# Two trunk layers on one core: the low part of the feed-forward weights made by an accumulating DMA instead of VectorE

## The chip, the cores and the metric

One core of a Trainium2 chip runs the whole program. The metric is the device time of one execution in microseconds; before the change it is 2593.01 us, the median of 2 runs (2591.31 to 2594.72).

## The reference

Two layers work on 640 tokens of 1024 channels (128 context tokens, 512 latent tokens). Each layer is

```
h += 1/2 * g1 * swiglu(adaLN1(h), ffn1)       # first feed-forward part
h += g2 * (heads(adaLN2(h)) @ w_out)          # mixer: state space, two attentions, Fourier
h += 1/2 * g3 * swiglu(adaLN3(h), ffn2)       # second feed-forward part

def swiglu(x, wg, wu, wd):
    return (jax.nn.silu(x @ wg) * (x @ wu)) @ wd
```

with wg and wu of 1024 x 2816 and wd of 2816 x 1024. The shift, scale and gate of each adaLN come from `silu(cond) @ w_mod + b_mod`, where w_mod is 1024 x 9216 per layer. Everything is float32.

## The kernel before, in words

**Products in three passes.** Each float32 operand is split into two parts of type float32r, a high part (the value rounded) and a low part (the value minus the high part). A product is three matmuls into the same PSUM tile: high x high, high x low, low x high (`mm3`, lines 257 to 265, and the same written out at lines 666 to 668 of `ffn`). The activations x and the hidden values (hh, hl) are split too. The tokens are worked in two halves of 256 and 384.

**The weight stream.** All weights of the feed-forward parts, of the input projection and of the output projection come as one stream of slabs, up to 1 MB each, loaded by SP into three `raw` buffers (`load_upto`). A slab of the gate and up weights holds 8 x 256 columns per partition, one of the down weights 4, 6 or 8 x 256. A slab gives two pieces, each a half of its columns, so a piece reads runs of 128 values (512 bytes) of the slab. `prep_to` (line 193) makes a piece: ScalarE writes the high part `whi` (line 209), VectorE the low part `wlo` (line 210), each contiguous per partition. The pieces lie in a ring of six slots. There are 344 pieces: per feed-forward part 44 of gate and up, and 32 (layer 0's first and second part) or 24 of down; 12 of the projection and 16 of the output per layer. A `raw` buffer is free for the next load when the low part of its second piece is made.

**Order of the work.** `ffn` goes through its chunks: for each of the 128 hidden channels of a chunk (a block: one gate and one up piece, 96 matmuls) both halves, then silu on ScalarE and the product and split on VectorE and ScalarE (lines 677 to 681), then the down product with `res_phase` (line 1551), which adds to the residual hT (line 595). Its last five blocks of channels are done half by half, so that the norm of the first half (`finish_half`, `rstd_from`, `x_prep`) can be made beside the second. `x_prep` (line 535) uses VectorE, ScalarE, and for some blocks POOL (line 561). Python code asks for the pieces ahead of their use (`w`, line 218, with `ahead` = 2); the order on each engine is then set by a scheduler with a timeline of its own, so instructions stand earlier or later than the code writes them.

**The modulation.** Beside the feed-forward parts VectorE multiplies slabs of w_mod (512 KB, tile `wm`) into `mvec` (lines 387 and 389). POOL issues their loads (line 353) into two buffers, so an issue waits until VectorE is done with the slab two before. They run in the first three of the four feed-forward parts; the last has none.

**The tables.** Beside the first chunks of two of the parts, tables of the state-space heads are made and written to DRAM by POOL's queue (tiles est, ft, zs).

Of the kernel before, what the change touches and what calls it, by code (L numbers as in the profile page):

```python
# [10 lines left out]
F32 = mybir.dt.float32  # L11
# [98 lines left out]
class Net:  # L110
    def __init__(self, tc, a, depth=DEPTH, dump=None):
        self.tc = tc
        self.nc = tc.nc
        self.a = a
        self.depth = depth
        self.dump = dump or {}
        self.es = ExitStack()
        self.n_act = 0
        self.wq = []
        self.raw = {}  # L120
        self.ready = {}
        self.i_use = 0
        self.i_prep = 0
        self.slabs = []
        self.i_load = 0
        self.slab_left = {}
        self.side = []
        self.job = None
        self.job_ns = 0
        self.chunks = CHUNKS  # L130
        self.limit = 0
        self.load_limit = 0
        self.seg = []
        self.mseq = [(l, gi, k) for l in range(depth) for gi in range(9) for k in range(DB)]
        self.m_load = 0
        self.m_use = 0
        self.mslab = {}
        self.mod_bufs = 4
        self.m_limit = 16
        self.m_pace = None  # L140
        self.m_ns = 0
        self.mod_then = None
        self.ahead = 2
        self.fine = False
        self.marks = ()
        self.x = [None, None]

    def pool(self, name, bufs=1, **kw):
# [17 lines left out]

# [1 line left out]
    def add_slab(self, src, pieces):  # L168
# [24 lines left out]
    def prep_to(self, n):  # L193
        while self.i_prep < min(n, len(self.wq), self.limit):
# [11 lines left out]
            with ExitStack() as es:  # L206
                for i in self.marks:
                    es.enter_context(self.tc.issue_after(i.ins))
                self.nc.scalar.activation(hv, v, AF.Copy)  # L209
                self.nc.vector.tensor_tensor(lv, v, hv, op=OP.subtract)  # L210
            self.ready[self.i_prep] = (hv, lv)
# [6 lines left out]
    def w(self, ahead=2):  # L218
        """Next operand of the stream; keeps `ahead` more in preparation."""
        i = self.i_use  # L220
# [3 lines left out]

# [1 line left out]
    def later(self, ns, f):  # L226
# [29 lines left out]

# [1 line left out]
    def mm3(self, out, pairs):  # L258
# [7 lines left out]

# [1 line left out]
    def setup(self):  # L268
# [36 lines left out]
    def setup_vectors(self):  # L305
        """small vectors: rows of 128, transposed to columns."""
        nc, a = self.nc, self.a
# [33 lines left out]

# [1 line left out]
    def mod_load(self, n):  # L343
# [14 lines left out]
    def mod_step(self):  # L358
        """One slab of w_mod: [128 rows, one of the nine vectors] on the tensor engine while it has nothing else,
        later [256 rows, half of one of the nine vectors] on the vector engine, the sum over partitions at the end."""  # L360
        nc = self.nc
# [66 lines left out]
    def mod_to(self, n, ns=None):  # L428
        """slabs up to n: spread over the coming ns, or what is left of them now."""
        self.m_limit = n  # L430
# [43 lines left out]

# [1 line left out]
    def load_x(self):  # L476
# [26 lines left out]
    def rstd_from(self, ss, c0, n):  # L503
        """ss [P, n] sums of squares per token -> rs_tok columns."""
        nc = self.nc
# [3 lines left out]

# [1 line left out]
    def norm_bc(self, half):  # L511
        """broadcast of rstd over the partitions, in PSUM [P, width]."""
        nc = self.nc
# [17 lines left out]
    def x_norm(self, half, rb, k, x):  # L531
        """h * rstd of one block."""
        self.nc.vector.tensor_tensor(x, self.hT[half][:, k, :], rb[:, 0:HALVES[half][1]], op=OP.mult)

    def x_prep(self, half, l, j, rb=None, xn=None):
        """x = h rstd A + B as two parts; xn: h rstd, where it is there already."""
        nc = self.nc
# [59 lines left out]
    def finish_half(self, half, l, j):  # L597
        """norm of a finished half of the residual, spread over the coming matmuls."""
        self.later(T_SUM, lambda: self.sq_sum(half))
# [8 lines left out]

# [1 line left out]
    def ffn_specs(self, l, nm, chunks):  # L610
# [21 lines left out]
    def ffn(self, l, j, nxt, chunks, e_pro=None):  # L632
        """j: 0 or 2; nxt: (layer, norm) the next phase reads, or None.
        e_pro: the pool of the tables that are made beside the first N_TAB chunks."""
        nc = self.nc
        hps, hp = self.open_pool("hp")
        nf = max(n for _, n in chunks[:N_TAB if e_pro else None])
        for ci, (c0, n) in enumerate(chunks):
# [58 lines left out]
            self.res_phase(n, [(hh[i], hl[i]) for i in range(2)], [(f, f) for f in range(n)], (l, j), nxt if last else None)  # L697
        hps.close()

# [1 line left out]
    def open_pool(self, name, **kw):  # L701
# [18 lines left out]

# [1 line left out]
    def ssm_tables(self, pro, l):  # L722
        """Generator: tables of layer l (E, intra-chunk Toeplitz blocks, F) to DRAM."""
        nc, a = self.nc, self.a
# [75 lines left out]
        def exp_fix(o, x):  # L800
            """e^x from the power of the rounded e and the rest of e."""
            stt(o, x, E_DELTA, zp, OP.mult, OP.mult)
            return tt(o, o, zp, OP.add)
# [57 lines left out]
        for n in (1, 2, 4):  # L861
# [9 lines left out]
            tt(yi, yi, tw[:, 0:n], OP.add)  # L871
        # (a - 1) / lambda
        nr = ts(T(), ap[:, 0, 1], -1.0, None, OP.add)
# [115 lines left out]

# [1 line left out]
    def proj_specs(self, l):  # L991
# [28 lines left out]
    def proj_u(self, l):  # L1020
        """u of the SSM, channels on the partitions, and u of the Fourier group, tokens on the partitions."""
        nc = self.nc
# [33 lines left out]

# [1 line left out]
    def ssm_init(self, l):  # L1058
# [18 lines left out]
    def ssm_te_load(self, l):  # L1077
        """most of E where the third part of the projection will be."""
        te = self.pp.tile([P, 10, 256], F32, name="te5", tag="P2")
# [49 lines left out]
    def ssm_y(self, l, mx):  # L1129
        """Generator over the steps after the scan."""  # L1130
        nc, a = self.nc, self.a
# [88 lines left out]

# [1 line left out]
    def merged_tiles(self):  # L1222
        self.mg = [self.x_tiles(h) for h in range(2)]

    def split(self, src, blk, c0, w, bias=None):
        """hi and lo parts of 128 channels of the merged heads, tokens c0..c0+w."""
        nc = self.nc
# [13 lines left out]

# [1 line left out]
    def fnet_load(self, l):  # L1243
# [53 lines left out]

# [1 line left out]
    def rope_tile(self, X, qr, ti):  # L1299
        """roped queries to qr, roped keys in place."""  # L1300
        nc = self.nc
# [60 lines left out]
    def qk_T(self, X, qr, ck, qt):  # L1362
        """Generator: transposes of queries and keys, four blocks of 128 columns per group.
        qt: roped q of the two query slots, roped k, plain q of the two slots, (ctx q, q, k, cached k)."""
        nc = self.nc
# [3 lines left out]
        def put(i, srcs, nq=4):  # L1369
            """the first nq blocks are queries: scaled by 1/8."""  # L1370
            pt = self.b([P, 4, P], name="qkT")
# [61 lines left out]
    def att(self, X, qt, blk0, mx, cv, PT, exs, sink=None, band=False):  # L1433
        """Latent queries; generator, yields where other work may go.
        PT: the two transposed tiles of a group; exs: function giving a tile for the exponentials."""
        nc = self.nc
# [80 lines left out]

# [1 line left out]
    def out_specs(self, l):  # L1519
# [18 lines left out]
    def out1(self, l):  # L1538
        """Generator: the part of the output projection whose heads are ready."""
        for db in range(DB):  # L1540
# [10 lines left out]
    def res_phase(self, n, xs, order, G, nxt, lead=1):  # L1551
        """y = W^T x, added to the residual, the last four blocks half by half."""
        def one(db, half, wd):
# [33 lines left out]

# [1 line left out]
    def sinks(self, l):  # L1589
# [8 lines left out]
    def mixer(self, l):  # L1598
# [35 lines left out]
        self.limit, self.load_limit = self.seg[l + 1]  # L1634
        # Fourier mixing while the scan runs
        rw = self.rawp.tile([P, RAW], F32, tag="raw", name="qs0")
# [4 lines left out]
        self.weave([self.fnet(l, mx), self.ax_norm(l), gq])  # L1641
        # both attention groups, the end of the state space heads, the first half of the output projection
        rw = self.rawp.tile([P, RAW], F32, tag="raw", name="qa0")
# [40 lines left out]
    def weave_main(self, main, others):  # L1684
        """others: (generator, one step every so many of main, offset)."""
        step = 0
# [15 lines left out]

# [1 line left out]
    def output(self, half):  # L1704
# [120 lines left out]
```

## Time and profile before

| | |
|---|---|
| median of 2 runs | 2593.01 us |
| the profiled execution's span | 2589.3 us |
| PE busy (matmul) | 2517.7 us (97%) |
| VectorE (DVE) busy | 1507.6 us (58%) |
| ScalarE (ACT) busy | 823.6 us (32%) |
| GpSimd (POOL) busy | 387.2 us (15%) |
| DMA queue q1 (issued by SP) | 193.30 MB, 23.7% of 16 engines' span |
| DMA queue q0 (issued by POOL) | 78.00 MB, 10.2% |
| granted TensorE clock, mean | 0.985 |

The profiled execution's own time is 2589.3 us from its first to its last instruction, 3.7 us below the median of the runs. Busy time of PE is modelled, since its matmuls overlap; DMA issues stand under the engine that issues them, and their transfers under the queue. "Idle before" in a group is the time that its engine stood still just ahead of it, with the engine, tile and line that ended it.

### The profile page before, as it was taken

The numbers are of one execution on the slowest core, as the hardware profiler recorded it, in microseconds if no ns is written. First come the engines' busy times: TensorE is split into PE (matmuls) and PEld (weight loads), VectorE is DVE, ScalarE is ACT, GpSimd is POOL, SyncE is SP. The second block draws the span as 40 slices with busy tenths as digits, with TensorE's granted clock in tenths as the row PEclk, the third lists the DMA queues.
The fourth block names the chain that finished last, engine by engine and source line by source line (L and its number), as shares of the span: only waits on it lengthen the run. The fifth ranks groups of instructions, "written<-read, shape, count | busy, mean of one in ns | idle before, by whom it ended". The sixth has DMA issues, their size and how long they took to land.

```text
span 2589.3 us, 41527 instructions
## 1 busy us (share of the span) xinstructions
PE 2517.7 (97%) x17054; PEld 2366.8 (91%) x17054; DVE 1507.6 (58%) x3012; ACT 823.6 (32%) x1547; POOL 387.2 (15%) x782
## 2 busy tenths in 40 slices
PE   5999999999899999999999999999999999999998
PEld 3899999998669899999999999999976799999998
DVE  6888677363667876454456666644546773333333
ACT  3332222242443532222233222223425553222222
POOL 2321111014801211000011001000183010000000
PEclk7999999999999999999999999999999999999999
DMA  7565444231114254333314445432401133222311
GB/s 254 158 182 183 145 147 147 90 101 55 34 35 147 58 168 126 119 111 114 114 50 143 137 125 151 139 106 66 126 18 54 34 98 98 69 82 62 98 49 41
DMA packets 199092, 273.93 MB, mean 106 GB/s; under 512 B 17208, under 2 KB 168472, under 8 KB 198392
## 3 DMA queue, kind: packets, MB, share of 16 engines
q1 hardware_dynamic: 176888, 193.30, 23.7%
q0 software_dynamic: 22016, 78.00, 10.2%
q8 instruction: 134, 2.20, 0.4%
q14 instruction: 54, 0.44, 0.1%
HBM read 256.29 MB, written 14.97 MB: 105 GB/s over the span
## 4 chain that ended last, share of the span: by engine, by line
PE 77%; issue 9%; POOL 7%; DVE 5%; DMA 2%; ACT 1%; SPq 0%; DVEq 0%; POOLq 0%; ACTq 0%
PE gu L261 14%; PE gu L263 14%; PE gu L262 14%; PE y L261 8%; PE y L262 8%; PE y L263 8%; POOL sc L1124 2%; POOL ee L1127 2%; POOL ee L1126 1%; DMA wm<-in_w_mod_dram 1%; POOL sc L1125 1%; DVE wlo L210 1%; DVE xt L551 1%; PE gu L668 1%; PE gu L666 1%
## 5 line engine op out<-in xcount | busy, mean ns | idle before, releaser
L261 PE MATMUL gu<-xh,whi 128*128 128x256 f32 (+1 forms) x2560 | 794.2, 310 | 0.9 <-DVE hx L679 0.9
L263 PE MATMUL gu<-xh,wlo 128*128 128x384 f32 (+1 forms) x2560 | 789.4, 309 | 0.6 <-DVE wlo L210 0.6
L262 PE MATMUL gu<-xl,whi 128*128 128x384 f32 (+1 forms) x2560 | 788.7, 308 | 0.0
L209 ACT ACTIVATE whi<-raw 128x1024 fp32r<-128x1024 f32 (+2 forms) x344 | 328.5, 960 | 875.4 <-PE gu L262 424.8
L210 DVE TENSOR_TENSOR wlo<-raw,whi 128x1024 fp32r<-128x1024 f32 (+2 forms) x344 | 380.2, 1107 | 343.3 <-ACT whi L209 342.9
L261 PEld LDWEIGHTS gu<-xh,whi 128*128 128x128 f32 x2560 | 481.3, 188 | 13.5 <-issue 11.0
L262 PEld LDWEIGHTS gu<-xl,whi 128*128 128x128 f32 x2560 | 482.6, 189 | 1.3 <-issue 1.2
L263 PEld LDWEIGHTS gu<-xh,wlo 128*128 128x128 f32 x2560 | 481.5, 188 | 1.6 <-DVE wlo L210 0.8
L261 PE MATMUL y<-hh,whi 128*128 128x384 f32 (+1 forms) x1408 | 436.0, 311 | 0.5 <-ACT est L957 0.3
L263 PE MATMUL y<-hh,wlo 128*128 128x384 f32 (+1 forms) x1408 | 434.8, 309 | 0.0
L262 PE MATMUL y<-hl,whi 128*128 128x384 f32 (+1 forms) x1408 | 434.6, 309 | 0.0
L389 DVE SCALAR_TENSOR_TENSOR mvec<-wm,cs,mvec 128x512 f32<-128x512 f32 x448 | 319.2, 750 | 20.9 <-DMA wm<-in_w_mod_dram 20.5
L595 DVE SCALAR_TENSOR_TENSOR hT<-y,G,hT 128x128 f32<-128x128 f32 (+1 forms) x432 | 175.8, 436 | 228.5 <-PE y L263 228.2
L261 PEld LDWEIGHTS y<-hh,whi 128*128 128x128 f32 x1408 | 266.1, 190 | 4.7 <-issue 3.7
L262 PEld LDWEIGHTS y<-hl,whi 128*128 128x128 f32 x1408 | 267.1, 190 | 0.5 <-issue 0.4
L263 PEld LDWEIGHTS y<-hh,wlo 128*128 128x128 f32 x1408 | 266.9, 190 | 0.0
L353 POOL DMA_DIRECT2D wm<-in_w_mod_dram x128 | 92.5, 723 | 956.7 <-DVE mvec L389 813.2
L679 DVE TENSOR_TENSOR hx<-sg,gu 128x256 f32<-128x256 f32 (+1 forms) x176 | 85.1, 483 | 119.5 <-ACT sg L677 119.2
L680 ACT ACTIVATE hh<-hx 128x256 fp32r<-128x256 f32 (+1 forms) x176 | 82.9, 471 | 184.6 <-DVE hx L679 184.5
L508 POOL TENSOR_TENSOR rst<-ms,mhalf 128x2 f32<-128x2 f32 (+1 forms) x12 | 11.2, 932 | 854.9 <-DVE ms L507 854.9
L677 ACT ACTIVATE sg<-gu 128x256 f32<-128x256 f32 (+1 forms) x176 | 75.3, 428 | 175.4 <-PE gu L263 170.8
L681 DVE TENSOR_TENSOR hl<-hx,hh 128x256 fp32r<-128x256 f32 (+1 forms) x176 | 86.3, 492 | 51.7 <-ACT hh L680 51.4
(313 smaller groups left out, 3239.8 us busy)
## 6 DMA issues: line engine op xcount, KB each, us to landing
wm<-in_w_mod_dram POOLq DMA_DIRECT2D x128, 512.0 KB, 4.2
raw<-in_ffn_w_gate_dram SPq DMA_DIRECT2D x44, 1024.0 KB, 5.4
raw<-in_ffn_w_up_dram SPq DMA_DIRECT2D x44, 1024.0 KB, 5.5
raw<-in_ffn_w_down_dram SPq DMA_DIRECT2D x24, 1024.0 KB, 5.2
raw<-in_ffn_w_down_dram SPq DMA_DIRECT2D x16, 768.0 KB, 4.9
raw<-in_w_in_dram SPq DMA_DIRECT2D x12, 1024.0 KB, 5.1
wm<-in_w_mod_dram SPq DMA_DIRECT2D x16, 512.0 KB, 5.5
raw<-in_ffn_w_down_dram SPq DMA_DIRECT2D x16, 512.0 KB, 4.1
```

Of the source, the lines that this page charges most:

```text
L209: self.nc.scalar.activation(hv, v, AF.Copy)
L210: self.nc.vector.tensor_tensor(lv, v, hv, op=OP.subtract)
L261: self.nc.tensor.matmul(out, wh, xh, start=(i == 0), stop=False)
L262: self.nc.tensor.matmul(out, wh, xl, start=False, stop=False)
L263: self.nc.tensor.matmul(out, wl, xh, start=False, stop=(i == n - 1))
L353: self.nc.gpsimd.dma_start(out=t.rearrange("p (j c) -> p j c", j=2), in_=w[kk * 256:(kk + 1) * 256, c0:c0 + 512].rearrange("(j p) c -> p j ...
L389: nc.vector.scalar_tensor_tensor(self.mvec[:, v], w, c, self.mvec[:, v], op0=OP.mult, op1=OP.add)
L595: nc.vector.scalar_tensor_tensor(h, y[:, s:e], G[:, k, v:v + 1], h, op0=OP.mult, op1=OP.add)
L677: nc.scalar.activation(sg[:, 0:w], g, AF.Silu)
L679: nc.vector.tensor_tensor(hx[:, 0:w], sg[:, 0:w], u, op=OP.mult)
L680: nc.scalar.activation(hh[half][:, f, :], hx[:, 0:w], AF.Copy)
L681: nc.vector.tensor_tensor(hl[half][:, f, :], hx[:, 0:w], hh[half][:, f, :], op=OP.subtract)
```

## The change

A flag `lo_dma` is set while `ffn` runs. With it, `prep_to` has ScalarE write the weights with turned sign (scale -1, rounded to float32r like the high part) into the low part's tile, and POOL issue a DMA that adds the weights from the `raw` slab to it. Without it (in the setup and the mixers) VectorE subtracts as before. The pieces that `ffn` asks for are 286 of the 344: all of the four parts but the first two, which the setup asks for, and the first of each layer's second part, which the mixer asks for; and the first of each layer's projection, which `res_phase` asks for at the end of the first part.

```diff
@@ __init__
+        self.lo_dma = False
@@ prep_to
                 self.nc.scalar.activation(hv, v, AF.Copy)
-                self.nc.vector.tensor_tensor(lv, v, hv, op=OP.subtract)
+                if self.lo_dma:
+                    self.nc.scalar.activation(lv, v, AF.Copy, scale=-1.0)
+                    self.nc.gpsimd.dma_start(out=lv.bitcast(F32), in_=v, accum_op=OP.add)
+                else:
+                    self.nc.vector.tensor_tensor(lv, v, hv, op=OP.subtract)
@@ ffn
         nc = self.nc
+        self.lo_dma = True
         hps, hp = self.open_pool("hp")
...
         hps.close()
+        self.lo_dma = False
```

The rest of the diff takes out comments and docstrings. Line numbers after line 146 move by one, after the new lines by five to seven.

The first place is POOL at the head of the first feed-forward part, where x is prepared (`xl`, made by lines 561 and 566) and the first slabs of w_mod (`wm`) are fetched. Before:

```order
L353 DMA wm<-in_w_mod_dram 128x2x512 x2
L561 TENSOR_TENSOR xl_566<-xt,xh_565 128x256 x6
L353 DMA wm<-in_w_mod_dram 128x2x512
L561 TENSOR_TENSOR xl_566<-xt,xh_565 128x256 x2
L561 TENSOR_TENSOR xl_608<-xt,xh_607 128x384 x4
```

After:

```order
L358 DMA wm<-in_w_mod_dram 128x2x512 x2
L566 TENSOR_TENSOR xl_566<-xt,xh_565 128x256 x6
L358 DMA wm<-in_w_mod_dram 128x2x512
L213 DMA wlo<-raw 128x8x128 x3
L358 DMA wm<-in_w_mod_dram 128x2x512
L566 TENSOR_TENSOR xl_566<-xt,xh_565 128x256 x2
L566 TENSOR_TENSOR xl_608<-xt,xh_607 128x384 x3
```

Three accumulating DMAs and a fetch now stand ahead of the last two subtractions of the first half of x and all of the second half.

The second place is POOL at the end of the same part, up to the norm of its first half (`rst`). Before:

```order
L353 DMA wm<-in_w_mod_dram 128x2x512 x2
L987 DMA tabm_102<-zs 16x8x128 x4
L353 DMA wm<-in_w_mod_dram 128x2x512 x36
L508 TENSOR_TENSOR rst<-ms,mhalf 128x2
L561 TENSOR_TENSOR xl_5394<-xt,xh_5393 128x256 x4
```

After:

```order
L358 DMA wm<-in_w_mod_dram 128x2x512
L213 DMA wlo<-raw 128x8x128 x2
L358 DMA wm<-in_w_mod_dram 128x2x512 x2
L213 DMA wlo<-raw 128x8x128
L358 DMA wm<-in_w_mod_dram 128x2x512 x2
L213 DMA wlo<-raw 128x8x128 x3
L358 DMA wm<-in_w_mod_dram 128x2x512 x2
L213 DMA wlo<-raw 128x8x128 x12
L513 TENSOR_TENSOR rst<-ms,mhalf 128x2
L566 TENSOR_TENSOR xl_5469<-xt,xh_5468 128x256 x4
```

Where 36 fetches of w_mod stood in a row, accumulating DMAs now stand between them, behind each fetch and its wait; the last twelve stand ahead of the norm.

The third place is VectorE at the head of layer 0's second feed-forward part, from the norm of the first half (`ms`, `diag`) through its x (`xt`, `xl`), beside the last residuals (hT) and squares (sq) of the second half. Before:

```order
L507 TENSOR_SCALAR ms<-pss 128x2
L210 TENSOR_TENSOR wlo<-raw,whi 128x1024
L578 TENSOR_TENSOR sq_8083<-sq_8083,sqt 128x384
L518 TENSOR_SCALAR diag<-ident,rst 128x128 x2
L595 SCALAR_TENSOR_TENSOR hT_71<-y,G_3162,hT_71 128x384
L210 TENSOR_TENSOR wlo<-raw,whi 128x1024
L551 SCALAR_TENSOR_TENSOR xt<-hT_70,A_4181,rbs 128x128 x8
L555 SCALAR_TENSOR_TENSOR xl_8311<-xt,modT_96,xh_8310 128x128
L595 SCALAR_TENSOR_TENSOR hT_71<-y,G_3162,hT_71 128x384
L555 SCALAR_TENSOR_TENSOR xl_8311<-xt,modT_96,xh_8310 128x128
L210 TENSOR_TENSOR wlo<-raw,whi 128x1024
L555 SCALAR_TENSOR_TENSOR xl_8311<-xt,modT_96,xh_8310 128x128
```

After:

```order
L512 TENSOR_SCALAR ms<-pss 128x2
L583 TENSOR_TENSOR sq_8158<-sq_8158,sqt 128x384
L523 TENSOR_SCALAR diag<-ident,rst 128x128 x2
L600 SCALAR_TENSOR_TENSOR hT_71<-y,G_3202,hT_71 128x384
L583 TENSOR_TENSOR sq_8158<-sq_8158,sqt 128x384
L556 SCALAR_TENSOR_TENSOR xt<-hT_70,A_4237,rbs 128x128 x8
L600 SCALAR_TENSOR_TENSOR hT_71<-y,G_3202,hT_71 128x384 x2
L560 SCALAR_TENSOR_TENSOR xl_8386<-xt,modT_96,xh_8385 128x128 x3
L556 SCALAR_TENSOR_TENSOR xt<-hT_70,A_4237,rbs 128x128 x2
```

The low parts are gone from between the steps of the norm; the rest stands in nearly the same order.

## Rows read from the trace of the kernel before

**Rows 1.** The page, part 1: engine, busy us, share of the span, instructions.
```profile
PE 2517.7 (97%) x17054; PEld 2366.8 (91%) x17054; DVE 1507.6 (58%) x3012; ACT 823.6 (32%) x1547; POOL 387.2 (15%) x782
```

**Rows 2.** The page, part 5: count | busy, mean ns | idle before, releaser.
```profile
L209 ACT ACTIVATE whi<-raw 128x1024 fp32r<-128x1024 f32 (+2 forms) x344 | 328.5, 960 | 875.4 <-PE gu L262 424.8 <-PE y L262 387.5 <-PE gu L668 18.4
L210 DVE TENSOR_TENSOR wlo<-raw,whi 128x1024 fp32r<-128x1024 f32 (+2 forms) x344 | 380.2, 1107 | 343.3 <-ACT whi L209 342.9
```

**Rows 3.** What PE waited for: us in total, times, longest us.
```profile
PE gu L263 <- DVE wlo L210: 0.6, 1, 0.6
PE gu L667 <- DVE wlo L210: 0.3, 1, 0.3
```

**Rows 4.** Windows, the feed-forward parts: length, then each engine's busy us, clock, DMA share.
```profile
62.00:545.00 483.00, 477.56 (x3316) 460.49 (x3315) 338.24 (x582) 136.09 (x234) 68.89 (x93) 0.99 0.47 144
846.00:1340.00 494.00, 489.01 (x3379) 478.24 (x3378) 296.35 (x599) 157.56 (x281) 51.92 (x68) 0.99 0.36 111
1340.00:1375.00 35.00, 35.00 (x249) 34.73 (x248) 17.17 (x31) 12.08 (x26) 8.25 (x7) 1.00 0.09 30
1375.00:1806.00 431.00, 430.60 (x2997) 422.74 (x2997) 255.73 (x433) 109.88 (x173) 31.09 (x43) 1.00 0.42 128
2104.00:2570.00 466.00, 463.02 (x3154) 462.09 (x3154) 173.27 (x284) 129.66 (x212) 10.96 (x11) 1.00 0.22 68
```

**Rows 5.** Timeline of DVE at the head of the second part: start, us, instruction.
```profile
848.59 1.22 DVE L210 TENSOR_TENSOR wlo<-raw,whi 128x1024 fp32r<-128x1024 f32 x1
...
852.87 1.23 DVE L210 TENSOR_TENSOR wlo<-raw,whi 128x1024 fp32r<-128x1024 f32 x1
...
857.00 1.21 DVE L210 TENSOR_TENSOR wlo<-raw,whi 128x1024 fp32r<-128x1024 f32 x1
```

**Rows 6.** Line 353, POOL's fetches of w_mod: ns min/median/max; what ended its waits.
```profile
L353 POOL DMA_DIRECT2D wm<-in_w_mod_dram x128: 704/722/790, 50.4 to 1702.3; - x128
...
  DVE mvec L389: 813.2, 107
```

**Rows 7.** The page, part 6: count, KB each, median us to landing.
```profile
wm<-in_w_mod_dram POOLq DMA_DIRECT2D x128, 512.0 KB, 4.2
raw<-in_ffn_w_gate_dram SPq DMA_DIRECT2D x44, 1024.0 KB, 5.4
```

**Rows 8.** Timeline of ACT in the first part, high parts two blocks apart.
```profile
407.46 1.06 ACT L209 ACTIVATE whi<-raw 128x1024 fp32r<-128x1024 f32 x1 [2.64 <-PE gu L262]
...
436.40 1.06 ACT L209 ACTIVATE whi<-raw 128x1024 fp32r<-128x1024 f32 x1 [2.64 <-PE gu L262]
```

**Rows 9.** The chain that ended last, head of the first part: start, us, what.
```profile
67.70 2.91 DVE wlo L210 x2
```

**Rows 10.** DMA from 2200 to 2300 us: queue, packets, MB, share of 16 engines.
```profile
q1 hardware_dynamic: 7372, 7.43, 24.5%
```

**Rows 11.** DMA from 197 to 206 us: queue, and the issues of that stretch.
```profile
q0 software_dynamic: 416, 1.31, 53.6%
...
tabm<-zs POOLq DMA_DIRECT2D x4, 64.0 KB, 3.7
```

**Rows 12.** DMA from 400 to 500 us: POOL's queue.
```profile
q0 software_dynamic: 1008, 3.67, 12.2%
```

**Rows 13.** Windows inside the first and third part: DMA share ahead of GB/s.
```profile
100.00:140.00 40.00, 39.82 (x282) 36.02 (x281) 35.48 (x68) 14.08 (x32) 9.82 (x16) 1.00 0.69 217
140.00:200.00 60.00, 59.69 (x426) 55.65 (x425) 53.34 (x95) 20.61 (x36) 12.55 (x21) 1.00 0.59 176
200.00:260.00 60.00, 60.00 (x425) 58.72 (x424) 48.10 (x89) 14.51 (x23) 8.87 (x14) 1.00 0.58 179
...
1375.00:1440.00 65.00, 64.60 (x447) 63.26 (x447) 44.14 (x70) 22.36 (x37) 5.82 (x8) 1.00 0.56 178
```

**Rows 14.** Timeline of POOL in the first part: start, us, instruction [idle before <-releaser].
```profile
440.82 0.72 POOL L353 DMA_DIRECT2D wm<-in_w_mod_dram  x1 [17.30 <-DVE mvec L389]
```

## The prediction, made before the changed kernel was run

> **What bounds the kernel now.** I read the page's table of engines first, then its groups of instructions, the list of waits, and the stages one by one. TensorE (PE) is busy in 2517.7 of 2589.3 us; VectorE (DVE), which the change relieves, in 1507.6; ScalarE (ACT), which gets new work, in 823.6; GpSimd (POOL), which gets new transfers, in 387.2 [rows 1]. The removed subtraction is a large group, 344 instructions of 1107 ns, 380.2 us [rows 2], but what counts is who waits for it: in the list of what PE waited for it stands twice, 0.6 and 0.3 us [rows 3]. So the change takes work off an engine that is not waited for. By stage: I call the feed-forward parts F1 (62 to 545 us), F2 (846 to 1375), F3 (1375 to 1806) and F4 (2104 on). In them PE is busy in 477.56 of 483, 524.01 of 529, 430.60 of 431 and 463.02 of 466 us [rows 4]; everything that any change to the making of weights could win there is 5.4 + 5.0 + 0.4 + 3.0 = 13.8 us.
>
> What it could cost is decided by the DMA engines: their share is 0.47 in F1, 0.36 in F2, 0.42 in F3, 0.22 in F4 [rows 4].
>
> **The change part by part.**
>
> *Removed.* 286 of the 344 subtractions (176 gate and up pieces and 112 down pieces, 288, of which the first two are made before F1 and one at the head of F2 and F4 each in the mixer, still on DVE; the first piece of each mixer, made at the end of F1 and F3, comes in). 286 x 1.107 = 317 us of DVE, down to about 1190. Beside PE work it is worth nothing. On the path it is worth something where DVE prepares x at the head of F2 and F4: three pieces stand between the steps of the norm of the first half, 1.22 us each [rows 5], and the order shows them gone. Counted by their spacing (1.13 each): -3.4 us twice, -7.
>
> *Added on ACT.* 286 sign-turned copies at the 960 ns of the copy beside them [rows 2]: 275 us, ACT to 1100 of 2590. ACT waits 424.8 + 387.5 us before the first copies for PE to free a slot [rows 2], so this time lies idle now. Its price on the path I bound by 0 and 10 us (one more 1.06 us instruction ahead of a silu, some ten times in 286) and take 0.
>
> *Added as a chain.* A low part is now there after two ACT copies (1.06 each), a POOL issue (0.72 [rows 6]) and a transfer. The transfer reads two operands of up to 512 KB and writes one; nearest is the load of 1024 KB, 5.4 us to landing [rows 7]. Sum 8.2 us, against 2.3 now. Is that hidden? ACT's first copies start at 407.46 and, two blocks on, at 436.40 us [rows 8]: a block of one gate and one up piece takes about 14.5 us, and each copy waits for PE, that is for a slot of the ring. The ring holds six pieces, three blocks; a piece is made when its slot is freed and used two blocks, 29 us, later. 8.2 fits. Only at the head of F1 does nothing lie between: there the chain of work runs through pieces being made, 2.91 us for two of them [rows 9], and on POOL three accumulating DMAs now stand ahead of the last steps of x (order, first place). I charge 8.2 - 2.3, and one issue each of two more: about +8 us. Between 0 and 15.
>
> *Added on the DMA engines.* This is the term that decides. In 100 us of F4 in which only weights are loaded, 7.43 MB in runs of 1 KB take a share of 24.5% [rows 10]: 3.30 us of all 16 engines per MB. The 286 pieces are 137.4 MB (222 of 512 KB, 32 of 384, 32 of 256), 34.3 MB in each part: one plain reading costs 34.3 x 3.30 = 113 us of the engines per part. No accumulating DMA stands in the trace, so let m be its price in plain readings. The DMA time in each part is then what the windows [rows 4] show plus 113 m:
> F1 227 + 113 m of 483; F2 181 + 113 m of 529; F3 181 + 113 m of 431; F4 103 + 113 m of 466.
> They fill up at m = 2.27, 3.08, 2.21 and 3.21. Bounds of m: 1 from below (it costs what a plain copy of its bytes does). From above by the transfers of 512-byte runs, the length that a half of a weight slab has: between 197 and 206 us POOL's queue moves 1.31 MB, four of 64 KB in such runs and the rest wm, in 53.6% of 9 us = 4.82 us [rows 11]; wm costs 12.2 us for 3.67 MB [rows 12], so 1.05 MB of it 3.49, and 0.26 MB in short runs 1.33: 5.1 us per MB, 1.54 readings. Twice that, for two operands, is m = 3.1. I take m = 2, two readings as the weights are read: the source is a weight slab in SBUF and the written side is a run of 4 KB, both nearer to that load [rows 10] than to a table written to DRAM in 512-byte runs.
> The Trainium skill ("Collectives: The Full Stack", section "The bandwidth ceiling") says that an add inside a DMA costs by its two source reads, half the rate of a copy, and not by the add; "DMA: Bandwidth & Descriptors" ("Why small descriptors are slow (HBM only)") says that SBUF to SBUF is spared the penalty of short runs. By them the sum is that of m = 2; no run here shows either.
> At m = 2 the parts are filled to 94, 77, 94 and 71%, but not evenly. At 100 to 140 us the share is 0.69 already, then 0.59 and 0.58 until 260; at 1375 to 1440 0.56 [rows 13]. With 2 x 113/483 = 0.47 (F3: 0.52) they need 1.16, 1.06, 1.05 and 1.08 of their time: 6.4 + 3.6 + 3.0 + 5.2 = +18 us if nothing is absorbed by the lead of two blocks. I take all of it.
>
> *Sum.* 2589.3 - 7 + 8 + 18 = 2608 as a span; the median of the runs shown lies 3.7 above this execution, so **2612 us**, +0.7%. About 2%, 52 us, is what a measurement of this kernel can tell from no change.
>
> **The rivals.**
>
> *The DMA engines become the bound (slower).* Same place, m above 2.2. For it: F1 and F3 stand at 94% by my own sum, and the only short runs of the trace cost 1.54. Against: the landings [rows 7], where a double load costs 1.2 us more to land than wm's 512 KB. At m = 3: F1 566, F2 520, F3 520, F4 442, so +83, 0, +89, 0, about 2775. At m = 3.1 about 2800; at m = 4 +196 + 104 + 202 + 89 = +591, about 3190; each further reading adds some 450.
>
> *POOL's queue holds the low parts up (slower).* POOL works in order, and its wm transfers wait for DVE to free a slab: 813.2 us in all [rows 6], once 17.30 at a stretch [rows 14]. An accumulating DMA behind one of them (order, second place) waits too, and behind it x's subtractions. 8.2 + 17.3 = 25.5 is still under 29; it decides from a landing of 8.9 us. With landings of 16 us, each long wait (one per 29 us in F1 to F3, some 50) would cost 7 us: 350, about 2960. The issues themselves are no bound: 286 x 0.72 = 206 us, and none of the 128 issues of wm took over 790 ns beside a busy DVE [rows 6]; at three times that POOL still has room.
>
> *The waits at the heads go altogether (faster).* DVE, freed of 317 us, prepares x and the modulation sooner and all 13.8 us of PE's idle time in the parts go: 2579. Against it: weights account for 0.9 us of what PE waits for [rows 3]. Faster by 52 us has no source in the profile unless the mixers gain, where nothing is changed but the first piece.
>
> **How the numbers follow.** Forecast 0.44 (0.41 within 2%, 0.03 slower), its own range 2580 to 2650; DMA bound 0.38, all slower by over 2%; POOL's queue 0.12 (0.11 slower); heads gone 0.06 (0.02 faster by over 2%, since I may miss a gain, 0.04 the same). Together: faster 0.02, within 2% 0.46, slower 0.52. The single likeliest case is still the forecast, and its time is the predicted one. The range reaches from 2580 to m = 4, 3200; above it lies dearer accumulation, about 0.14, and below it 0.03.
>
> **What would show it.** Right: DVE about 1190 us, ACT about 1100; POOL's accumulating group 286 strong at about 0.7 to 1 us; landings of 5 to 9 us; DMA share near 0.94 in F1 and F3 and 0.7 to 0.8 in F2 and F4; PE waiting for the accumulating DMA by about 20 us in all, between 100 and 260 us and after 1375. Wrong: DMA share at 1.0 over whole parts with landings far above 10 us and PE waiting in every block (first rival); DMA share low but POOL waiting for mvec with PE waiting behind it (second); or F4, which has no wm, slowed as much as F1, which would mean a price per transfer that I don't know.

## The result and the profile after

The changed kernel takes 2695.54 us (median of 2 runs, 2686.67 and 2704.41) against 2593.01: a ratio of 1.0395, 95% interval 1.0313 to 1.0478. It is slower by about 4%. The prediction's point, 2612, forecast no measurable change; its range, 2580 to 3200, holds the result.

The page of the changed kernel, engines, DMA queues and the two groups that replace the subtraction (rows 1 and 2 have those of before):

```profile
PE 2562.2 (95%) x17054; PEld 2399.9 (89%) x17054; DVE 1210.4 (45%) x2726; ACT 1059.3 (39%) x1833; POOL 818.7 (30%) x1068
...
q0 software_dynamic: 294880, 215.38, 53.1%
q1 hardware_dynamic: 176888, 193.30, 22.7%
...
L213 POOL DMA_DIRECT2D wlo<-raw x286 | 438.2, 1549 | 1133.4 <-ACT wlo L212 857.3 <-ACT mev L416 109.8 <-ACT hh L686 30.8
L212 ACT ACTIVATE wlo<-raw 128x1024 fp32r<-128x1024 f32 (+2 forms) x286 | 278.2, 973 | 22.1 <-PE gu L673 22.1
```

The work moved as the change says: 286 pieces, DVE down by 297 us, ACT up by 236. But one issue of an accumulating DMA holds POOL for 1549 ns, twice a wm issue [rows 6], and q0 carries 137.4 MB more (215.38 against 78.00), at five times the share of the engines. The list of issues, with the median us to landing in the last column [rows 7]:

```profile
wlo<-raw POOLq DMA_DIRECT2D x222, 512.0 KB, 8.0
wm<-in_w_mod_dram POOLq DMA_DIRECT2D x128, 512.0 KB, 6.6
raw<-in_ffn_w_gate_dram SPq DMA_DIRECT2D x44, 1024.0 KB, 7.1
raw<-in_ffn_w_up_dram SPq DMA_DIRECT2D x44, 1024.0 KB, 9.3
```

A low part lands in 8.0 us, and the other transfers of these parts got slower with it: wm 6.6 for 4.2, the gate weights 7.1 for 5.4, the up weights 9.3 for 5.5. The windows of the four parts in the changed kernel (length, busy us of PE, PEld, DVE, ACT, POOL, clock, DMA share, GB/s) answer to rows 4:

```profile
62.00:577.00 515.00, 483.34 (x3312) 466.26 (x3311) 263.69 (x504) 193.73 (x308) 179.25 (x168) 0.97 0.99 202
879.00:1445.00 566.00, 537.47 (x3629) 521.58 (x3628) 242.88 (x562) 230.91 (x386) 179.68 (x158) 0.97 0.90 166
1445.00:1887.00 442.00, 433.68 (x2993) 425.66 (x2992) 178.46 (x359) 164.82 (x236) 128.19 (x104) 0.99 1.00 195
2201.00:2694.00 493.00, 477.26 (x3233) 474.67 (x3233) 104.41 (x231) 189.57 (x283) 111.31 (x77) 0.99 0.82 137
```

F1 and F3 are full (0.99, 1.00); F2 and F4 are not (0.90, 0.82), and are longer all the same. To see where time is lost I compare one instruction that both kernels run twelve times: POOL's reciprocal root of a norm (tile rst), at the end of each part and at each head. Timeline of POOL, before (start, us, instruction):

```profile
538.87 0.71 POOL L508 TENSOR_TENSOR rst<-ms,mhalf 128x2 f32<-128x2 f32 x1 [94.53 <-DVE ms L507]
...
865.53 0.85 POOL L508 TENSOR_TENSOR rst<-ms,mhalf 128x3 f32<-128x3 f32 x1 [2.91 <-DVE ms L507]
...
1349.51 0.86 POOL L508 TENSOR_TENSOR rst<-ms,mhalf 128x3 f32<-128x3 f32 x1 [5.92 <-DVE ms L507]
1802.34 0.71 POOL L508 TENSOR_TENSOR rst<-ms,mhalf 128x2 f32<-128x2 f32 x1 [99.36 <-DVE ms L507]
...
2102.18 1.62 POOL L508 TENSOR_TENSOR rst<-ms,mhalf 128x2 f32<-128x2 f32 x1 [132.21 <-DVE ms L507]
2121.85 0.85 POOL L508 TENSOR_TENSOR rst<-ms,mhalf 128x3 f32<-128x3 f32 x1 [3.06 <-DVE ms L507]
```

and after:

```profile
571.02 0.71 POOL L513 TENSOR_TENSOR rst<-ms,mhalf 128x2 f32<-128x2 f32 x1 [15.60 <-DVE ms L512]
...
913.98 0.87 POOL L513 TENSOR_TENSOR rst<-ms,mhalf 128x3 f32<-128x3 f32 x1 [5.66 <-DVE ms L512]
...
1419.05 0.87 POOL L513 TENSOR_TENSOR rst<-ms,mhalf 128x3 f32<-128x3 f32 x1 [2.83 <-DVE ms L512]
1883.14 0.71 POOL L513 TENSOR_TENSOR rst<-ms,mhalf 128x2 f32<-128x2 f32 x1 [15.60 <-DVE ms L512]
...
2198.45 1.37 POOL L513 TENSOR_TENSOR rst<-ms,mhalf 128x2 f32<-128x2 f32 x1
2229.30 0.87 POOL L513 TENSOR_TENSOR rst<-ms,mhalf 128x3 f32<-128x3 f32 x1 [2.97 <-DVE ms L512]
```

The differences, and what each stretch adds to them (the last mark is 2581.91 before, 2694.85 after; of the 16.4 us up to the head of F2, the first mixer has 0.4 and the head itself, from the norm of its first half to that of its second, 15.9):

| mark | later by, us | added since the mark above |
|---|---|---|
| end of F1 | 32.1 | 32.1 |
| head of F2, second half | 48.5 | 16.4 |
| end of F2 | 69.5 | 21.0 |
| end of F3 | 80.8 | 11.3 |
| end of the second mixer | 96.3 | 15.5 |
| head of F4, second half | 107.5 | 11.2 |
| end | 112.9 | 5.4 |

Not all of this is waiting. PE's busy time is 44.5 us longer (2562.2 for 2517.7) for the same 17054 matmuls, at a mean granted clock of 0.966 for 0.985; 15.3 of the 44.5 lie in the second mixer (below), some 28 in the four parts.

F4's head costs 11.2 us within 31 us, all the rest of F4 5.4. Over the whole part the DMA share is 0.82, but in these 31 us it is 1.00:

```profile
2198.45:2229.30 30.85, 20.85 (x134) 19.33 (x133) 13.34 (x35) 14.79 (x33) 10.85 (x11) 0.89 1.00 154
```

ACT's timeline there shows how the time is lost:

```profile
2208.92 0.75 ACT L563 ACTIVATE xt<-xt,modT 128x128 f32<-128x128 f32 x2
2220.33 1.06 ACT L210 ACTIVATE whi<-raw 128x1024 fp32r<-128x1024 f32 x1 [10.66 <-DMA raw<-in_ffn_w_up_dram]
2221.29 0.39 ACT L559 ACTIVATE xh<-xt,modT 128x128 fp32r<-128x128 f32 x1
...
2231.95 0.49 ACT L528 ACTIVATE rbs<-rb 128x384 f32<-128x384 f32 x1 [6.59 <-PE rb L526]
```

ACT stands 10.66 us at a high-part copy, because the weights of that slab have not arrived; behind it, in ACT's order, stand the preparation of x and the squares of the norm, for which the timeline shows no other wait. The load was issued just ahead of ACT's coming to it (at 2209.67 us), and ACT could start only 11.2 us after the issue:

```profile
2209.09 0.37 SPq L190 DMA_DIRECT2D raw<-in_ffn_w_up_dram  x1
```

The same in sum, from the lists of what each engine waited for (us, times, longest), after:

```profile
ACT whi L210 <- DMA raw<-in_ffn_w_up_dram: 185.6, 24, 14.4
DVE mvec L394 <- DMA wm<-in_w_mod_dram: 142.5, 41, 10.0
...
PE gu L673 <- DMA wlo<-raw: 18.3, 6, 4.4
PE gu L268 <- DMA wlo<-raw: 9.6, 3, 5.5
...
SPq L190 <- DMA wlo<-raw: 1851.6, 166, 47.1
```

PE waits for the low parts themselves 27.9 us (0.9 before [rows 3]). The last row points to the reason for ACT's 185.6: SP loads a slab into one of three raw buffers, and a buffer is now free only when the accumulating DMA that reads it has landed. That SP waits is not new; before, it waited about as long, for VectorE's low part:

```profile
SPq L189 <- DVE wlo L210: 1790.3, 150, 41.1
```

New is who frees the buffer, and how late. This gave two theories. A: the transfers are dear, and the engines are full. B: they are not too many but too late, so that raw buffers and operands come late at the heads. C (ACT's extra copies) and D (POOL's order and its issues) are the others.

### The profile page after: what moved, and what is told of

The parts are those of the page before. It is cut to its first block, busy times and chain, and to the rows that moved or that the text cites. A ratio compares the mean times of both kernels' runs of the same rounds, so it can differ in the third digit from the quotient of the medians.

```text
span 2702.6 us, 42229 instructions
## 1 busy us (share of the span) xinstructions
PE 2562.2 (95%) x17054; PEld 2399.9 (89%) x17054; DVE 1210.4 (45%) x2726; ACT 1059.3 (39%) x1833; POOL 818.7 (30%) x1068
## 3 DMA queue, kind: packets, MB, share of 16 engines
q0 software_dynamic: 294880, 215.38, 53.1%
## 4 chain that ended last, share of the span: by engine, by line
PE 59%; DMA 15%; issue 11%; POOL 9%; DVE 4%; ACT 2%; SPq 0%; POOLq 0%; ACTq 0%; DVEq 0%
PE gu L268 10%; PE gu L266 10%; PE gu L267 10%; PE y L266 6%; PE y L267 6%; PE y L268 6%; DMA wm<-in_w_mod_dram 5%; DMA raw<-in_ffn_w_up_dram 4%; DMA wlo<-raw 4%; POOL wlo L213 2%; PE O L1506 1%; POOL ee L1134 1%; POOL ee L1133 1%; POOL sc L1131 1%; PE S L1465 1%
## 5 line engine op out<-in xcount | busy, mean ns | idle before, releaser
L268 PE MATMUL gu<-xh,wlo 128*128 128x256 f32 (+1 forms) x2560 | 791.6, 310 | 9.7 <-DMA wlo<-raw 9.6
L267 PE MATMUL gu<-xl,whi 128*128 128x256 f32 (+1 forms) x2560 | 792.0, 309 | 0.0
L213 POOL DMA_DIRECT2D wlo<-raw x286 | 438.2, 1549 | 1133.4 <-ACT wlo L212 857.3
L394 DVE SCALAR_TENSOR_TENSOR mvec<-wm,cs,mvec 128x512 f32<-128x512 f32 x448 | 318.3, 758 | 142.6 <-DMA wm<-in_w_mod_dram 142.5
L212 ACT ACTIVATE wlo<-raw 128x1024 fp32r<-128x1024 f32 (+2 forms) x286 | 278.2, 973 | 22.1 <-PE gu L673 22.1
L358 POOL DMA_DIRECT2D wm<-in_w_mod_dram x128 | 107.7, 854 | 398.8 <-DVE mvec L394 268.4
```

The source lines that it names most:

```text
L212: self.nc.scalar.activation(lv, v, AF.Copy, scale=-1.0)
L213: self.nc.gpsimd.dma_start(out=lv.bitcast(F32), in_=v, accum_op=OP.add)
L267: self.nc.tensor.matmul(out, wh, xl, start=False, stop=False)
L268: self.nc.tensor.matmul(out, wl, xh, start=False, stop=(i == n - 1))
L358: self.nc.gpsimd.dma_start(out=t.rearrange("p (j c) -> p j c", j=2), in_=w[kk * 256:(kk + 1) * 256, c0:c0 + 512].rearrange("(j p) c -> p j ...
L394: nc.vector.scalar_tensor_tensor(self.mvec[:, v], w, c, self.mvec[:, v], op0=OP.mult, op1=OP.add)
```

## The experiments

Each ratio is to the kernel before on the same chip, with its 95% interval.

**x1_micro: the price of one transfer.** Seven stages with nothing beside them, one execution.

```diff
+        for i in range(24):
+            nc.gpsimd.dma_start(out=D[:, i], in_=src(i), accum_op=OP.add)
...
+            nc.gpsimd.dma_start(out=Df[:, i], in_=Sf[:, 1024 * (i % 2):1024 * (i % 2) + 1024], accum_op=OP.add)
...
+            nc.gpsimd.dma_start(out=D[:, i], in_=src(i))
```

> Not the network but seven stages with nothing else beside them, each on a cleared tile (all of the network's work is left out, the outputs hold the tile): 24 accumulating transfers of 512 KB with 512-byte source runs as in the feed-forward; 24 accumulating with 4 KB runs; 24 plain copies with 512-byte runs issued by POOL; the same issued by SP; 12 weight loads of 1 MB; 6 loads beside 12 accumulating; then 4 accumulating and 4 plain ones one behind the other. Theory A (the accumulating transfer is bound by the bytes that the engines move, at the prediction's 2 readings): 24 of them end in about 24 x 3.46 = 83 us. Theory B (throughput is not what counts, the latency of one and of a load beside them is): lone accumulating transfers land in 4 to 8 us, and a load beside them lands in over 9 us against 4 to 6 alone. If the transfers cost what the packet times of the changed kernel's profile say (2.6 readings): 24 in about 108 us. Theory D (POOL's issue is the limit): stages 1 to 3 each last 24 x 1.5 = 37 us or as long as their issue, and the stage by SP is shorter.

POOL's timeline once its queue is full (start, us held, instruction, idle before): accumulating from 512-byte runs (L131), from 4 KB runs (L135), and plain from 512-byte runs (L139):

```profile
89.00 1.55 POOL L131 DMA_DIRECT2D D<-S  x1 [2.79 <-issue]
93.34 1.55 POOL L131 DMA_DIRECT2D D<-S  x1 [2.79 <-issue]
97.66 1.55 POOL L131 DMA_DIRECT2D D<-S  x1 [2.78 <-issue]
...
177.78 0.86 POOL L135 DMA_DIRECT2D D<-S  x1 [1.80 <-DMA D<-S]
180.44 0.86 POOL L135 DMA_DIRECT2D D<-S  x1 [1.80 <-DMA D<-S]
...
275.02 0.88 POOL L139 DMA_DIRECT2D D<-S  x1 [1.15 <-DMA D<-S]
277.22 0.89 POOL L139 DMA_DIRECT2D D<-S  x1 [1.31 <-DMA D<-S]
```

The spacing is the price of 512 KB (0.524 MB): 4.34 us (93.34 - 89.00), 2.66 and 2.20. In the prediction's unit, 3.30 us per MB [rows 10], 4.34 us is 4.34 / (0.524 x 3.30) = 2.5 plain readings. All 24 took 106.5 us (28.93 to 135.40, when the next clearing starts). Theory A's 83 is too low, the 108 of the dearer reading holds. Theory D falls for this stage: POOL spends 1.55 of each 4.34 us on its issue, and the plain copies took 57.1 us issued by POOL and 51.3 by SP. One at a time, accumulating (L159) and plain (L161), and loads beside accumulating (L152; alone their median was 11.8):

```profile
L159 POOL DMA_DIRECT2D D<-S x4: 1547/1547/1547, 551.2 to 571.6; - x4
...
DMA to landing us min/median/max: 6.4/6.4/6.4
...
L161 POOL DMA_DIRECT2D D<-S x4: 882/890/913, 578.5 to 590.9; - x4
...
DMA to landing us min/median/max: 3.8/3.8/3.8
...
DMA to landing us min/median/max: 5.5/17.8/25.5
```

So B's premises hold too: a lone one takes 6.4 us, and loads land later beside them (17.8 for six of them queued beside twelve accumulating transfers, against 11.8 for twelve queued alone).

**x2_act_only: the second copy without the DMA.**

```diff
-                    self.nc.gpsimd.dma_start(out=lv.bitcast(F32), in_=v, accum_op=OP.add)
+                    self.nc.vector.tensor_tensor(lv, v, lv, op=OP.add)
```

> ACT still makes the sign-turned copy of each piece, but VectorE adds the weights onto it, so there is no accumulating DMA. Theories A and B (the DMA is what costs, by throughput or by the latency that it adds to raw loads and operands): the loss goes, 2585 to 2615 us. Theory C (ACT's second copy of 0.97 us per piece, 275 us in all, delays the x preparation and the silu that stand behind it in ACT's order): the loss stays, over 2650 us.

2598.72 against 2587.34, ratio 1.0049 (1.0028 to 1.0070). ACT's copies cost 11.4 us; the other 90 or so are the DMA's. C falls as the main cause.

**x4_head12: the heads by VectorE.**

```diff
+                self.n_lo += 1
-                if self.lo_dma:
+                if self.lo_dma and self.n_lo > HEAD:
```

> The change, but the first 12 pieces of each feed-forward part get their low part from VectorE as before; the other 238 of the 286 go by DMA. Theory A (throughput): a sixth of the traffic goes, so at most a sixth of the loss, 2675 to 2700 us. Theory B (the loss is at the heads, where the ring is empty and PE waits for each operand as it comes): half of the loss or more goes, 2615 to 2650 us, and PE is not stopped by the low part at the head of the second and fourth part.

2632.49, ratio 1.0172 (1.0147 to 1.0197): a sixth of the pieces taken off the DMA gives back over half of the loss, as B says. By the marks F4 lost 0.1 us, F3 1.2, F2's head 0.1, the rest of F2 11.7, but F1 22.1 (of the kernel's 48.9 at the last mark, 16.8 lie in the second mixer, while the first mixer gave 3.1 back). The windows of F1 and F4 in this kernel:

```profile
62.00:565.00 503.00, 480.87 (x3300) 463.11 (x3299) 272.28 (x516) 185.57 (x296) 165.25 (x156) 0.98 0.92 196
...
2150.00:2632.00 482.00, 476.86 (x3258) 475.41 (x3259) 118.69 (x249) 184.04 (x277) 97.67 (x68) 1.00 0.72 127
```

F4 has its head back and loses nothing at a share of 0.72. F1, at 0.92 over all (and 1.12 from 150 to 200 us, 1.20 from 250 to 300, a share above 1 meaning that packet times overlap), still loses 22: there the engines are full well behind the head, as A says (x8 below tells how far A goes there).

**x5_half and x6_plain_copy: half of the transfers; cheaper transfers.** The first sends every second piece by DMA. The second leaves the accumulation out, so that the low part is the raw weights; the number and size of its transfers, their order and the waits are those of the change.

```diff
-                if self.lo_dma:
+                if self.lo_dma and self.n_lo % 2 == 0:
...
-                    self.nc.gpsimd.dma_start(out=lv.bitcast(F32), in_=v, accum_op=OP.add)
+                    self.nc.gpsimd.dma_start(out=lv.bitcast(F32), in_=v)
```

> Every second piece of the weights by the accumulating DMA (n_lo counted from each part's start), the others by VectorE as before, so half of the transfers, spread evenly, the heads included. The lone stages measured 4.34 us of all engines per accumulated 512 KB, so 286 of them take 310 us of each part; half of them leave the first part at about 0.8 full. Theory A (the engines' time): the loss goes but for half of ACT's 11 us, 2595 to 2615 us. Theory B (latency of each operand and raw load at the heads): a third of the loss or more stays, 2625 to 2660.

> Each accumulating DMA becomes a plain copy onto the same tile: same transfers, same order, same waits, but nothing is added (the low part is the raw weights, so the sum is left out). Alone such a copy took 2.20 us per 512 KB against 4.34, landed in 3.8 us against 6.4, and its issue held POOL 0.89 us against 1.55. Theory A: the first part's engines are then at 0.77, the loss falls to 10 to 30 us, 2600 to 2625. Theory B: it falls as the landings of the raw loads fall. Theory D (POOL in its order, the wait chain as such, whatever the price of one transfer): the loss stays, over 2650.

x5: 2604.33 against 2593.84, ratio 1.0027 (1.0002 to 1.0052). x6: 2596.47, 1.0016 (0.9990 to 1.0041). Both are within half a per cent of before. In x6 a low part lands in 4.8 us and ACT's waits for the up weights are 33.0 us in place of 185.6. POOL's order, the raw buffers held by a transfer and the longer chain are all still there and cost next to nothing: D falls, and B is no cause by itself. The price of a transfer is what starts the loss. (x6 also holds POOL 0.88 us per issue for 1.55; the issue's own share isn't separated.)

**x7_contiguous: the whole change, from 4 KB runs.**

```diff
-            src = w[:, f0 * P:(f0 + n) * P].rearrange("(k p) f -> p k f", p=P)
-            return src, [P, DB, n * P]
+            src = [(w[:, (f0 + i) * P:(f0 + i + 1) * P].rearrange("(k p) f -> p k f", p=P), i) for i in range(2)]
+            return src, [P, 2, DB, P]
```

and the same for w_down, with pieces `v[:, 0]` and `v[:, 1]`.

> The whole change, but each slab of raw weights is loaded as its two pieces, each 4 KB in one run on a partition, by two loads of 512 KB in place of one of 1 MB. Alone an accumulating transfer from 4 KB runs took 2.66 us against 4.34 from 512-byte runs. Theory A: 286 of them take 190 us of each part and not 310, all parts fit, 2605 to 2640 us (the upper end if the loads with half the run length, and twice as many, cost more). If the run length doesn't matter beside other traffic: 2680 to 2710.

2630.61 against 2593.84, ratio 1.0135 (1.0088 to 1.0182): inside A's 2605 to 2640. Nearly two thirds of the loss go, though the loads are now twice as many and have runs half as long. (POOL's issue falls with the run length too, to 0.86 us; how much of the gain is the issue's isn't separated.)

**x8_raw_free: the raw buffers free early.** The DMA reads a resident tile, so the low part's sum is left out. (The direct test, a fourth raw buffer, x3_four_raw, has no result: with it 13.66 KB per partition of SBUF are left where a later pool needs 20.)

```diff
-                    self.nc.gpsimd.dma_start(out=lv.bitcast(F32), in_=v, accum_op=OP.add)
+                    src = self.rope[:, 0:1, :].to_broadcast([P, k, w])
+                    self.nc.gpsimd.dma_start(out=lv.bitcast(F32), in_=src, accum_op=OP.add)
```

> The accumulating DMA reads 512-byte runs of a small tile that is always there, not the raw weights (so the low part is wrong and its sum left out): same number, size and run length of transfers, but a raw buffer is free as soon as ACT has made its two copies. Theory B (a raw buffer held until the transfer lands delays the next load, and ACT stands at its high-part copy): a large part of the loss goes, under 2650 us, and ACT's waits for raw loads fall under 90 us. Theory A: no gain, 2675 to 2710.

2648.05 against 2593.84, ratio 1.0209 (1.0167 to 1.0250). Nearly half of the loss goes at the same number, size and run length of transfers, where A expected no gain, 2675 to 2710. What ACT and SP waited for in this kernel:

```profile
ACT whi L210 <- DMA raw<-in_ffn_w_up_dram: 9.9, 6, 4.2
...
SPq L190 <- ACT wlo L212: 1450.5, 117, 27.3
```

SP now waits for ACT's copy and no longer for the transfer, and ACT's 185.6 us of waiting are 9.9. So the held buffer is shown as the cause of these waits: it turns dear transfers into late loads, and those into an ACT that stands.

By the marks F1 lost 13.8 us for 32.1, F2's head 4.7 for 15.9, F4's head 6.2 for 11.2, F3 5.2 for 11.3. So of F1's loss, too, more goes (18.3) than stays. In the changed kernel ACT waits in F1:

```profile
ACT whi L210 <- DMA raw<-in_ffn_w_up_dram: 58.2, 7, 14.4
```

and in x8 not at all for these loads. The transfers of F1 were no quicker to land in x8 (low parts 8.9 us for 8.3, loads 8.8 for 7.8, medians), at a share of 0.98. One rival is left: the packets of POOL's queue took some 7% less time in x8 (50.5% of 2650.4 us against 53.1% of 2702.6). Packet times overlap, so this is no price by itself, but the resident tile may be cheaper to read, and how much of the gain is that is not shown.

**x9_contig_head12 and x10_free_long_runs: two of the edits together.** x9 joins x7 and x4. x10 is x8 with 2 KB runs of the resident tile (the sum left out again).

```diff
-                    src = self.rope[:, 0:1, :].to_broadcast([P, k, w])
+                    src = self.rope.rearrange("p a n -> p (a n)")[:, 0:k * w // 2].rearrange("p (o n) -> p o n", o=1).to_broadcast([P, 2, k * w // 2])
...
```

> Contiguous pieces as in the run before (4 KB runs for the accumulating transfers, two loads of 512 KB per slab), and the first 12 pieces of each part by VectorE. If the loss has two parts, full engines in the first part (22 us stayed there with the head by VectorE, 9 us with contiguous pieces) and late operands and raw loads at the heads, both go: 2595 to 2618 us, what is left being ACT's copies, some 10 us, and the mixer's clock. If one cause lay under both, it stays near 2630.

> The accumulating DMA reads a small resident tile again (raw buffers free early, sum left out), but in runs of 2 KB and not 512 bytes, with the weight loads as they are in the change. Against the same kernel with 512-byte runs (2648 us) this changes the price of a transfer alone. Theory A (price of the transfers by their run length): 2600 to 2625 us. If the rest of that loss is the lateness of each operand whatever the transfer's price: 2640 to 2655.

x9: 2614.30 against 2588.52, ratio 1.0080 (1.0052 to 1.0108), inside the 2595 to 2618 expected if the loss has two parts. x10: 2623.28, ratio 1.0145 (1.0128 to 1.0162): within A's 2600 to 2625, and 19 us less over before than x8. (Part of the gap may be the second mixer's clock: of the 33.8 us between the two profiled runs 8.9 lie in F1 and 10.0 in that mixer.) In x9 DVE still waits for wm:

```profile
DVE mvec L399 <- DMA wm<-in_w_mod_dram: 96.7, 36, 6.5
```

and the kernel loses 0.8%, so most of the 142.5 us of that wait in the changed kernel need not be on the path. No version tried beats the kernel before.

**The second mixer.** 15.5 of the 112.9 us lie in a stage that the change doesn't touch. PE's order there is the same; the windows from the end of F3 to the end of that mixer, before and after, differ in the clock (0.98, 0.93), and PE is busy 15.3 us longer for the same work:

```profile
1802.34:2102.18 299.84, 289.81 (x1842) 241.32 (x1842) 185.81 (x444) 127.90 (x292) 96.06 (x269) 0.98 0.22 68
```

```profile
1883.14:2198.45 315.31, 305.13 (x1841) 251.89 (x1841) 185.36 (x442) 129.33 (x293) 94.51 (x270) 0.93 0.21 64
```

Runs of one kernel fall in two groups some 15 us apart: x9's took 2599.09 and 2601.52 us at mean clocks of 0.986 and 0.983, the other three 2614.30 to 2617.25 at 0.976 or 0.977. x6 shows that the accumulating transfers are not needed for it: its profiled run (2606.07, with three more of its ten from 2608.89 to 2610.30, the others 2590.36 to 2596.52) lost 17.9 us in this mixer and nothing in sum elsewhere. The two runs of the changed kernel (2686.67, 2704.41) differ likewise, and the profiled one is the longer. Why the clock falls there in some runs is open.

## Why the prediction was wrong in its point and held in its range

- **The price m.** The step that failed is "I take m = 2". Measured: 2.5, inside the bounds of 1 and 3.1. The forecast rested on m staying under 2.21, so the first rival, the DMA engines as the bound, was the case that came nearest, and the prediction's own chances stood at 0.52 for slower. Of that rival's signs the shares came, but the landings (8.0 us) and PE's waits did not. With 2.5 the prediction's own sum has F1 at 227 + 283 = 510 of 483 and F3 at 464 of 431: +27 and +33 for its +18, that is about 2654. The DMA shares of the four parts give m between 2.3 and 2.9 by the same sum. F1 lost 32.1 for 27, F3 only 11.3 for 33. That F1 fits looks like luck: with the raw buffers free early (x8) F1 loses 13.8 and F3 5.2, so the sum, in which nothing is absorbed by the lead of two blocks, seems too high for full engines alone. (In the sum of the first rival the times are 2766 at m = 3 and 2790 at 3.1 by its own terms, not 2775 and 2800.)
- **Run length.** I put the 512-byte runs of the source aside because the written side is a run of 4 KB. x1 says otherwise: 4.34 us from 512-byte runs, 2.66 from 4 KB. The Trainium skill's sentence that SBUF to SBUF is spared the penalty of short runs ("DMA: Bandwidth & Descriptors", "Why small descriptors are slow (HBM only)") does not hold for these accumulating transfers: 1.63 times. The Trainium skill's rule that an add in a DMA runs at half a copy's rate ("Collectives: The Full Stack", "The bandwidth ceiling"), which that page gives for the reduce step of a ring of cores, agrees with 4.34 against 2.20 for 512-byte sources, 1.97 times; from 4 KB runs it is 1.21 times the same plain copy (a plain one from 4 KB runs was not run).
- **What no term had.** F1 and F3 are 43.4 of the 112.9 us; the rest fell where the sum had 0: 15.9 at F2's head, 16.0 in its body, 5.1 at the head of F3 (between the norms of its two halves), 15.5 in the second mixer, 11.2 at F4's head and 5.4 behind it. The change lets the DMA, not DVE, release the raw buffer, and I counted only the wait for the low part (29 us of lead against 8.2). The wait of the next load for the buffer, and of the x preparation behind ACT's high-part copy, were not costed. x8 gives back 11.2 us at F2's head, 5.0 at F4's and 18.3 in F1; x4 the two heads whole. That PE would be busy some 28 us longer in the parts, at a lower clock, was in no term either. "F4 slowed as much as F1" was my sign of a price per transfer: F4 lost 16.6, half of F1's, and two thirds of it at its head.
- **+8 at the head of F1.** Of the right size: with the first 12 pieces by VectorE (x4) F1 loses 10.0 us less, in which the price of these transfers is contained.
- **ACT's 275 us at 0, bounds 0 to 10.** x2 measured 11.4 (7 to 18): just above the upper bound, which its interval includes.
- **-7 at the heads.** Not seen: in x6, where nothing is late, F2's head is no earlier against the end of F1 than before.
- **POOL.** An issue was taken at 0.72 us; it is 1.55. The second rival's mechanism did not come: the median landing of 8.0 stays under its 8.9 (the longest took 17.1), POOL's waits for DVE at the wm slabs fell from 813.2 us to 268.4, and x6, with the same order, loses nothing.
- **What was to be seen.** DVE 1210 for 1190, ACT 1059 for 1100, landings of 8.0 in 5 to 9 and PE's waits of 27.9 for 20 came about; the shares did not (0.99, 0.90, 1.00 and 0.82 for 0.94, 0.77, 0.94 and 0.71). Of the waits for the low part 18.3 us lay at the heads and none between 100 and 260 us; PE stood there all the same, for DVE and ACT (between 100 and 250 us it is busy 138.5 of 150).

## What to carry to other kernels

When work goes from an engine to a DMA, price the transfer by its own kind (accumulating, run length) before summing, and lay its source out contiguously: here the same transfer cost 4.34 or 2.66 us. Then ask which buffer it now holds and which in-order engine stands at the load into that buffer; nearly half of the loss went when the buffer came free early. A part's average share hides its head: F4's was full for 31 us in a part at 0.82. Work taken off an engine that nobody waits for has little to win: here PE stood idle for 13.8 us in all four parts.

## What was not expected of the hardware

- An accumulating DMA of 512 KB from 512-byte runs went as 512-byte packets (24960 for 24 transfers), a plain one from the same runs, issued by POOL, as 3456 packets in all: the accumulating form keeps the short pieces.
- Its issue holds POOL 1.55 us from 512-byte runs and 0.86 from 4 KB runs, and with the queue full POOL issues one per 4.34 us; at 29.8 us from issue to landing (x1, median) that is about seven under way, an estimate.
